# The key group ahead of the indexer's queries, page fetches one megabyte at a time, and a bit search that picks one of two prepared words

## The chip, the core and the metric

The kernel runs on one core of one Trainium2 chip. The time is device microseconds of one execution; lower is better. The kernel before was timed in three runs; a profiled execution, with its own time, gives the rows further down.

## The reference

One inference step of a two-layer decoder runs for 256 prompt tokens and for 8 sample sequences of 4 new tokens each, 288 tokens in all. Layer 0 mixes tokens by sparse attention, layer 1 by a Conformer convolution; each is followed by a convolutional FFN. Only the attention layer is touched here. Cut to what matters:

```python
p = x @ w_in            # 2048 -> q 2048 | k 512 | v 512 | qi 1024 | ki 64 | wi 16
q, k, qi, ki = partial rotary of each
dots  = einsum('thd,sd->ths', qi, ki)                      # 16 index heads of 64
score = einsum('th,ths->ts', wi * scale, relu(dots))
idx   = top_k(where(causal, score, -inf), k_sel)           # 64 of 256 (prompt), 256 of 2052 (sample)
o     = softmax(q . k[idx]) v[idx];  y = o @ w_out
```

For the samples `ki` consists of 2048 cached rows per sequence, on 16 pages of 128 rows that a page table names, and 4 new ones. The cached keys and values are gathered by the selected index.

## The kernel before

All activations stand transposed, features on partitions and the 288 tokens along the row. Every weight GEMM is done in three fp32r matmuls per tile: weights and activations are each split into a high and a low part, and the products high-high, low-high and high-low are summed in PSUM (lines 227 to 229). A `Slab` is 512 KB of weights. `pump` (line 134) works ahead of PE: it issues slab loads on SP's queue up to five ahead into the `raw` ring, and splits slabs up to two beyond the current one: `wh` on ACT (line 158), `wl` as raw minus wh on VectorE (line 160), or on GpSimd where `s.pool` is set. That is so for the first two of the four attention query groups (lines 545 to 547). PE, ACT, VectorE, GpSimd and SP each run what they are given in order.

The order is written by hand, by credits. `gemm` yields after some matmuls the PE time that they stand for (0.3675 for three), and `tick` (line 166) adds it to each of several `Lane`s: `ev` (what follows a group's evacuation), `bg` (page loads, then the sample's index work), `bg2` (preparations and the first half of the prompt's index). A lane is a queue of generators; while its credit is positive its next piece is emitted into the engines' programs, and the number that the piece yields is taken off the credit. So a `yield 1.4` says: give PE 1.4 us of GEMM before the next piece. A credit is capped at 3. `drain` emits at once whatever is left in a lane. With `k.fine` set, GEMMs tick after every three or six matmuls, otherwise after each column block.

The attention layer's groups come in this order: an 80-column group (`ki` and `wi`), two groups of index queries `qi`, the group of keys `k`, four groups of queries `q`, two of `v`. A 512-column group is 8 slabs, 192 matmuls, 23.52 credits. `k.fine` is set ahead of the `k` group.

Around them:

- **Pages.** Lines 658 to 669: four indirect gathers on GpSimd's DMA queue each bring 1 MB of index pages (128 pages, a quarter of the features) into a `kvt` tile, and four stores put them into a DRAM buffer `kid`. The program order on GpSimd is gather 0, 1, 2, store 0, gather 3, store 1, 2, 3; a store waits for its gather. `load_kx` (line 671) then reads `kid` back, transposed, in eight loads of 512 KB issued on ACT, one per sequence; each needs all four stores. The first comes after `KXD[0]` = 30 credits, the others `KXD[1]` = 3 apart.
- **Index of the samples.** `sample_index` (line 801) follows `load_kx` in `bg`. It waits until the second `qi` group is rotated (`rope_qi`, line 697), does all dots with the cached rows (line 833), and sums them into a score row `S` of 516 columns on 128 partitions (four strips of each of 32 tokens).
- **The search.** Lines 878 to 895 find each token's 256th largest score, bit by bit, 31 bits. One bit is: count the scores at or above the candidate (line 881, VectorE, with an accumulator), sum the four strips by a PE matmul (`total`, line 861), compare with 256 into `fb`, the bit's value if the count suffices (line 893, from PSUM), and candidate `nx ^ fb` (line 895). Beside that `v ^ fb` (line 884) and the next `nx` (line 888) are made. `v`, `nx`, `fb`, `cand` are words of 128x1.
- **Compaction.** Lines 896 to 980: ties are ranked, the selected columns are moved together in nine predicated steps (lines 938 to 946) and shifted by strip in eight (lines 965 to 972); a PE matmul adds the strips (line 975), `idxS` is written (line 978), and `kv_load` starts gathers of keys and values. Then the second half of the prompt's index goes on (`prompt_index(1)`, line 985): 16 top-k rounds on VectorE (lines 1029 to 1033), 8 over 128 and 8 over 256 columns, 2.6 credits each.
- **Keys and queries.** `evac_rope` (line 704) copies a group's PSUM out on ACT and puts the rotation into `ev`. The `k` group also stores its output through SP.

After the four `q` groups everything left is drained (line 1068), then come the two `v` groups (line 1085) and the attention loop over 32 sample tokens. The rest of the kernel follows in one stream of GEMMs.

Of the kernel before, what the change touches and what calls it, by code (L numbers as in the profile page):

```python
# [7 lines left out]
F32 = mybir.dt.float32  # L8
# [9 lines left out]
NT = 16  # L18
# [27 lines left out]
CQ = 287  # L46
KXD = (30.0, 3.0)
PEM, NACT = 3, 4
BIS = (1.4, 0.2)
ROPE = 0.5  # L50
# [482 lines left out]
def trunk(ctx, tc, a, o, stages=9):  # L533
# [5 lines left out]
    win, wout = a["w_attn_in"], a["w_attn_out"]  # L539
    g_idx = [k.add(Group([(win, KIC, 80)], [80], NT, 8))]  # L540
    g_idx += [k.add(Group([(win, QIC + 512 * i, 512)], [128] * 4, NT, 2)) for i in range(2)]
    g_k = k.add(Group([(win, KC, 512)], [128] * 4, NT, 2))
    g_q = [k.add(Group([(win, QC + 512 * i, 512)], [128] * 4, NT, 2)) for i in range(4)]
# [120 lines left out]

    for i in range(6):
        if i < 4:
            gather(kx[i], kq, pgq[:, i:i + 1])
        if i >= 2:
            nc.gpsimd.dma_start(kid[:, 2048 * i - 4096:2048 * i - 2048], kx[i - 2])

# [130 lines left out]
    def sample_index():  # L801
# [47 lines left out]
        nc.vector.tensor_copy(S[:, :512], sc[:, :512])  # L849
        yield 1.5  # L850
        p = pb()
# [26 lines left out]
        for bit in range(30, -1, -1):  # L878
            cnt = sp.tile([128, 1], F32, name="cnt", bufs=2)
            scr = sp.tile([128, W1], I16, name="scr", bufs=2)  # L880
            nc.vector.tensor_scalar(scr, S, cand.bitcast(F32), 0.0, op0=OP.is_ge, op1=OP.add, accum_out=cnt)
            if bit < 30:
                w = word("v")
                nc.vector.tensor_tensor(w, v, fb, op=OP.bitwise_xor)
                v = w
            if bit:
                nx = word("nx")
                nc.vector.tensor_scalar(nx, v, 1 << (bit - 1), None, op0=OP.bitwise_xor)
            yield BIS[0]
            p = total()  # L890
            yield BIS[1]
            fb = word("fb")
            nc.vector.tensor_scalar(fb, p[:, :1], float(KSEL_S), float(1 << bit), op0=OP.is_ge, op1=OP.mult)
            cand = word("cand")
            nc.vector.tensor_tensor(cand, nx if bit else v, fb, op=OP.bitwise_xor)
        v = cand
# [41 lines left out]
        for b in range(9):  # L938
            s_ = 1 << b
            m = sp.tile([128, 512], I32, name="m_", tag="w", bufs=3)  # L940
            nc.vector.tensor_scalar(m, x_, 1 << (15 + b), None, op0=OP.bitwise_and)
            y = sp.tile([128, 512], I32, name="x_", tag="w", bufs=3)
            nc.vector.scalar_tensor_tensor(y, m, 0.0, x_, op0=OP.is_equal, op1=OP.mult)
            nc.vector.copy_predicated(y[:, :512 - s_], m[:, s_:], x_[:, s_:])
            x_ = y
            yield 2.2

# [15 lines left out]
        nc.vector.tensor_copy(lst, xi)  # L963
        yield 2.2
        for b in range(8):
# [5 lines left out]
            lst = y  # L971
            yield 1.2
        p = pb()
# [65 lines left out]

    k.bg2.append(prepare())  # L1040
    for gi in range(2):
        ps = k.gemm(g_idx[gi + 1], xin, pg)
# [3 lines left out]
        if gi == 0:  # L1046
# [4 lines left out]

    k.fine = True
    kT = ap.tile([128, NKV, T], F32, name="kT")
    vt = ap.tile([128, 2, 512], F32, name="vt")
    vs = ap.tile([32, 512], F32, name="vs")
    q = base.tile([128, NT, T], F32, name="x")
    qn = ap.tile([128, NKV, NS * TS, GQ], F32, name="qn")
    ps = k.gemm(g_k, xin, pg)
    evac_rope(0, ps, [kT[:, m] for m in range(4)],
              lambda: nc.sync.dma_start(o["k"].rearrange("(j p) t -> p j t", p=128), kT))  # L1060

# [793 lines left out]
```

## Time and profile before

| | |
|---|---|
| three runs, median (lowest to highest) | 2680.12 us (2676.99 to 2683.59) |
| the profiled execution, its own time | 2690.26 us |
| its span | 2688.5 us |
| PE busy | 2565.7 us (95%) |
| VectorE (DVE) busy | 1650.9 us (61%) |
| ScalarE (ACT) busy | 1160.8 us (43%) |
| GpSimd (POOL) busy | 619.6 us (23%) |
| DMA | 454.90 MB, 169 GB/s on the mean |

PE is the matmul stream, PEld its weight loads, which overlap it. The busy share of PE says little about a single stage: its idle stretches are short and lie mostly in the attention layer, so the rows below are taken from the first 345 us. "Idle before" in brackets names what ended an engine's idle time. A letter q behind an engine (SPq, ACTq) marks its DMA issues. The granted clock is a share of PE's full clock: 1.00 is the higher of its two levels, 0.50 the lower. Matmul records are missing here and there.

### The profile page before, as it was taken

Reading aid. Unit: us, or ns where it says so; the run is one execution under the profiler, and the core shown is the slowest. Engines: PE = TensorE matmul, PEld = TensorE weight load, DVE = VectorE, ACT = ScalarE, POOL = GpSimd, SP = SyncE. Lnnn points to the kernel's source line nnn. Section 1 sums busy time; section 2 is a strip of 40 time slices with the busy share of each in tenths; the row PEclk is TensorE's granted clock in tenths of the full one; section 3 lists DMA queues with packets and bytes.
Section 4 is the critical chain, followed back from the end, with each engine's and each line's share of the span. In section 5 each row is a group of like instructions: output and inputs, shape, how many; then the busy total and the mean of one; then the engine's idle time right before and its main releaser. Section 6 shows DMA issues by size and latency. Waiting matters only on the chain.

```text
span 2688.5 us, 49542 instructions
## 1 busy us (share of the span) xinstructions
PE 2565.7 (95%) x19608; PEld 2460.0 (92%) x19608; DVE 1650.9 (61%) x2544; ACT 1160.8 (43%) x1801; POOL 619.6 (23%) x857
## 2 busy tenths in 40 slices
PE   6888888999999999999999999899999999999997
PEld 5677865999999999999999889899999999999997
DVE  4479643668566445555557888778655544555554
ACT  3333343446444334444345544656444333444334
POOL 2023233143122110101135454443111000111123
PEclk8899999999999999999999999999999999999998
DMA  9533666555554555555544767455555445555643
GB/s 325 118 103 117 226 219 232 176 162 184 181 161 154 176 162 168 161 172 159 170 159 132 195 159 184 165 163 157 173 162 168 163 160 165 171 166 159 171 164 106
DMA packets 410552, 454.90 MB, mean 169 GB/s; under 512 B 34816, under 2 KB 338608, under 8 KB 409168
## 3 DMA queue, kind: packets, MB, share of 16 engines
q1 hardware_dynamic: 389600, 396.46, 47.8%
q0 software_dynamic: 12400, 51.09, 5.6%
q10 hardware_dynamic: 8320, 4.19, 0.8%
q8 instruction: 153, 2.51, 0.4%
q14 instruction: 79, 0.65, 0.1%
HBM read 438.37 MB, written 13.30 MB: 168 GB/s over the span
## 4 chain that ended last, share of the span: by engine, by line
PE 79%; DVE 3%; POOL 2%; issue 1%; ACT 1%; DMA 1%; SPq 0%; ACTq 0%; DVEq 0%; POOLq 0%
PE pt L229 25%; PE pt L228 25%; PE pt L227 25%; PE tr L1181 1%; PE pt L1641 1%; DVE wl L160 1%; PE m L1245 1%; PE sc L1202 1%; POOL x L485 0%; PE q L1153 0%; ACT wh L158 0%; DMA xt<-spread 0%; PE tr L1131 0%; DMA kvx<-kvc,idxS 0%; DVE cy L1687 0%
## 5 line engine op out<-in xcount | busy, mean ns | idle before, releaser
L160 DVE TENSOR_TENSOR wl<-raw,wh 128x1024 fp32r<-128x1024 f32 (+2 forms) x709 | 885.3, 1251 | 795.1 <-ACT wh L158 781.8
L158 ACT ACTIVATE wh<-raw 128x1024 fp32r<-128x1024 f32 (+1 forms) x726 | 760.5, 1051 | 949.7 <-PE pt L228 692.7
L229 PE MATMUL pt<-xh,wl 128*128 128x288 f32 (+1 forms) x3520 | 1040.5, 296 | 4.8 <-DVE wl L160 4.8
L227 PE MATMUL pt<-xh,wh 128*128 128x288 f32 (+1 forms) x3520 | 1042.6, 296 | 0.8 <-ACT xh L1300 0.8
L228 PE MATMUL pt<-xl,wh 128*128 128x288 f32 (+1 forms) x3520 | 1042.7, 296 | 0.1
L229 PEld LDWEIGHTS pt<-xh,wl 128*128 128x128 f32 x3520 | 666.5, 189 | 6.4 <-DVE wl L160 6.4
L227 PEld LDWEIGHTS pt<-xh,wh 128*128 128x128 f32 x3520 | 663.7, 189 | 7.8 <-issue 5.3
L228 PEld LDWEIGHTS pt<-xl,wh 128*128 128x128 f32 x3520 | 664.1, 189 | 0.5 <-DVE xl L1301 0.3
L229 PE MATMUL pt<-hh,wl 128*128 128x288 f32 (+1 forms) x1664 | 495.5, 298 | 2.9 <-DVE wl L160 2.9
L227 PE MATMUL pt<-hh,wh 128*128 128x288 f32 (+1 forms) x1664 | 493.2, 296 | 1.2 <-ACT wh L158 1.2
L228 PE MATMUL pt<-hl,wh 128*128 128x288 f32 (+1 forms) x1664 | 494.1, 297 | 0.0
L229 PEld LDWEIGHTS pt<-hh,wl 128*128 128x128 f32 x1664 | 312.8, 188 | 3.9 <-DVE wl L160 3.9
L227 PEld LDWEIGHTS pt<-hh,wh 128*128 128x128 f32 x1664 | 313.5, 188 | 2.3 <-ACT wh L158 2.1
L228 PEld LDWEIGHTS pt<-hl,wh 128*128 128x128 f32 x1664 | 313.8, 189 | 0.2
L1416 POOL COPY sto<-gpad 128x2 f32<-128x2 f32 x88 | 82.0, 931 | 963.5 <-ACT gpad L1409 963.4
L227 PE MATMUL pg<-xh,wh 128*128 128x288 f32 (+1 forms) x464 | 144.1, 311 | 15.9 <-ACT wh L158 13.7
L229 PE MATMUL pg<-xh,wl 128*128 128x288 f32 (+1 forms) x464 | 140.3, 302 | 3.7 <-DVE wl L160 3.2
L228 PE MATMUL pg<-xl,wh 128*128 128x288 f32 (+1 forms) x464 | 140.2, 302 | 0.1
L1420 ACT ACTIVATE s<-y,pvec 128x304 f32<-128x304 f32 x88 | 48.4, 550 | 162.0 <-DVE y L1415 162.0
L227 PEld LDWEIGHTS pg<-xh,wh 128*128 128x128 f32 (+1 forms) x464 | 89.3, 193 | 19.2 <-ACT wh L158 14.1
L302 POOL TENSOR_TENSOR lns<-lns,x 128x288 f32<-128x288 f32 x56 | 52.8, 944 | 184.3 <-DVE x L1329 176.8
L229 PEld LDWEIGHTS pg<-xh,wl 128*128 128x128 f32 (+1 forms) x464 | 89.3, 192 | 5.6 <-DVE wl L160 5.6
(386 smaller groups left out, 2447.5 us busy)
## 6 DMA issues: line engine op xcount, KB each, us to landing
raw<-w_ffn_gate SPq DMA_DIRECT2D x352, 256.0 KB, 2.9
raw<-w_ffn_up SPq DMA_DIRECT2D x352, 256.0 KB, 3.2
raw<-w_ffn_down SPq DMA_DIRECT2D x169, 512.0 KB, 3.6
raw<-w_attn_in SPq DMA_DIRECT2D x64, 512.0 KB, 4.3
raw<-w_pw SPq DMA_DIRECT2D x128, 256.0 KB, 4.7
raw<-w_attn_out SPq DMA_DIRECT2D x32, 512.0 KB, 4.7
raw<-w_pw SPq DMA_DIRECT2D x32, 512.0 KB, 4.2
xt<-spread SPq DMA_DIRECT2D x60, 136.0 KB, 2.8
```

The lines of the kernel that those rows point to most:

```text
L158: nc.scalar.activation(wh[:, :n], r[:, :n], AF.Copy)
L160: eng.tensor_tensor(wl[:, :n], r[:, :n], wh[:, :n].bitcast(F32), op=OP.subtract)
L227: nc.tensor.matmul(out, wh[:, c:c + w], xh, start=st, stop=False)
L228: nc.tensor.matmul(out, wh[:, c:c + w], xl, start=False, stop=False)
L229: nc.tensor.matmul(out, wl[:, c:c + w], xh, start=False, stop=sp)
L302: nc.gpsimd.tensor_tensor(self.s1, self.s1, self.x[:, j], op=OP.add)
L1181: nc.tensor.transpose(p[:, h * 128:(h + 1) * 128], g[:, h * 128:(h + 1) * 128], ident)
L1202: nc.tensor.matmul(p[32 * h:32 * h + 16, :KSEL_S], qz[b % 2][:, i, h], kt[:, h], start=False, stop=(i == TS - 1), skip_group_check=True)
L1245: nc.tensor.matmul(po[32 * h:32 * h + 16, :128], z[:, c, i, h], g[:, 512 + h * 128:640 + h * 128], start=False, stop=(i == TS - 1 and c == ...
L1416: nc.gpsimd.tensor_copy(sto[:, j, 0:2], gp[:, 256:258])
L1420: nc.scalar.activation(s[:, :304], y[:, :304], AF.Silu, bias=k.par(bc, j))
L1641: nc.tensor.matmul(p[32 * i:32 * i + 32, :TP], dg[:, i, m - PEM], xt[:, i, 4 * (m - PEM):4 * (m - PEM) + TP], start=m == PEM, stop=m == 7, ...
```

## The change

Three things are edited, and the credits with them.

1. The group of keys comes right behind the 80-column group, in the list of slabs (so in the order of weight loads) and in the program; `k.fine` and the tiles of keys and values move up with it. The two index-query groups follow, then the four query groups. `sample_index` now starts beside the first query group.
2. On GpSimd's queue each page gather is followed at once by its store, so the order is gather 0, store 0, gather 1, store 1, and so on. The first read-back comes after 42 credits, the others 4.2 apart.
3. In the search, two candidates are made from the current one by XOR with constants, one for each outcome of the bit's test; the test's flag picks by a predicated copy. `v` and the product with the bit's value are gone.

The credits: 1.3 for 1.4 in the search's first wait of a bit, 0.5 for 1.5 behind the score sum, 2.4 for 2.2 per compaction step, 1.2 for 2.2 ahead of the list, 1.3 for 1.2 per list step.

```diff
-KXD = (30.0, 3.0)
+KXD = (42.0, 4.2)
-BIS = (1.4, 0.2)
+BIS = (1.3, 0.2)
...
     g_idx = [k.add(Group([(win, KIC, 80)], [80], NT, 8))]
+    g_k = k.add(Group([(win, KC, 512)], [128] * 4, NT, 2))
     g_idx += [k.add(Group([(win, QIC + 512 * i, 512)], [128] * 4, NT, 2)) for i in range(2)]
-    g_k = k.add(Group([(win, KC, 512)], [128] * 4, NT, 2))
...
-    for i in range(6):
-        if i < 4:
-            gather(kx[i], kq, pgq[:, i:i + 1])
-        if i >= 2:
-            nc.gpsimd.dma_start(kid[:, 2048 * i - 4096:2048 * i - 2048], kx[i - 2])
+    for i in range(4):
+        gather(kx[i], kq, pgq[:, i:i + 1])
+        nc.gpsimd.dma_start(kid[:, 2048 * i:2048 * i + 2048], kx[i])
...
         nc.vector.tensor_copy(S[:, :512], sc[:, :512])
-        yield 1.5
+        yield 0.5
...
             nc.vector.tensor_scalar(scr, S, cand.bitcast(F32), 0.0, op0=OP.is_ge, op1=OP.add, accum_out=cnt)
-            if bit < 30:
-                w = word("v")
-                nc.vector.tensor_tensor(w, v, fb, op=OP.bitwise_xor)
-                v = w
-            if bit:
-                nx = word("nx")
-                nc.vector.tensor_scalar(nx, v, 1 << (bit - 1), None, op0=OP.bitwise_xor)
+            below = 1 << bit >> 1
+            no, yes = word("no"), word("yes")
+            nc.vector.tensor_scalar(no, cand, 1 << bit | below, None, op0=OP.bitwise_xor)
+            nc.vector.tensor_scalar(yes, cand, below, None, op0=OP.bitwise_xor)
             yield BIS[0]
             p = total()
             yield BIS[1]
-            fb = word("fb")
-            nc.vector.tensor_scalar(fb, p[:, :1], float(KSEL_S), float(1 << bit), op0=OP.is_ge, op1=OP.mult)
-            cand = word("cand")
-            nc.vector.tensor_tensor(cand, nx if bit else v, fb, op=OP.bitwise_xor)
+            fl = word("fl")
+            nc.vector.tensor_scalar(fl, p[:, :1], float(KSEL_S), None, op0=OP.is_ge)
+            nc.vector.copy_predicated(no, fl, yes)
+            cand = no
...
             nc.vector.copy_predicated(y[:, :512 - s_], m[:, s_:], x_[:, s_:])
             x_ = y
-            yield 2.2
+            yield 2.4
...
         nc.vector.tensor_copy(lst, xi)
-        yield 2.2
+        yield 1.2
...
             lst = y
-            yield 1.2
+            yield 1.3
...
     k.bg2.append(prepare())
+
+    k.fine = True
+    kT = ap.tile([128, NKV, T], F32, name="kT")
+    vt = ap.tile([128, 2, 512], F32, name="vt")
+    vs = ap.tile([32, 512], F32, name="vs")
+    qn = ap.tile([128, NKV, NS * TS, GQ], F32, name="qn")
+    ps = k.gemm(g_k, xin, pg)
+    evac_rope(0, ps, [kT[:, m] for m in range(4)],
+              lambda: nc.sync.dma_start(o["k"].rearrange("(j p) t -> p j t", p=128), kT))
+
     for gi in range(2):
         ps = k.gemm(g_idx[gi + 1], xin, pg)
...
     k.bg.append(sample_index())
 
 
-    k.fine = True
-    kT = ap.tile([128, NKV, T], F32, name="kT")
-    vt = ap.tile([128, 2, 512], F32, name="vt")
-    vs = ap.tile([32, 512], F32, name="vs")
     q = base.tile([128, NT, T], F32, name="x")
-    qn = ap.tile([128, NKV, NS * TS, GQ], F32, name="qn")
-    ps = k.gemm(g_k, xin, pg)
-    evac_rope(0, ps, [kT[:, m] for m in range(4)],
-              lambda: nc.sync.dma_start(o["k"].rearrange("(j p) t -> p j t", p=128), kT))
```

## Rows read from the trace of the kernel before

**Rows 1.** The page's part 4, the chain that ended last: share of the span by engine.

```profile
PE 79%; DVE 3%; POOL 2%; issue 1%; ACT 1%; DMA 1%; SPq 0%; ACTq 0%; DVEq 0%; POOLq 0%
```

**Rows 2.** Busy time in six stretches. Columns: stretch (us), its length, then for PE, PEld, DVE, ACT and POOL the busy us with the number of instructions, the granted PE clock, the DMA share, GB/s.

```profile
18.00:55.60 37.60, 30.54 (x201) 28.76 (x200) 15.77 (x26) 11.91 (x15) 11.10 (x20) 0.91 1.01 399
72.00:95.00 23.00, 23.00 (x175) 23.00 (x174) 8.41 (x9) 7.23 (x8) 0.00 (x0) 1.00 1.00 209
95.00:109.50 14.50, 4.11 (x28) 3.46 (x27) 9.22 (x18) 2.92 (x6) 0.00 (x0) 0.72 0.96 213
144.00:229.50 85.50, 68.94 (x493) 64.56 (x491) 73.54 (x203) 27.78 (x42) 33.61 (x15) 1.00 0.38 116
229.50:280.00 50.50, 41.74 (x303) 40.49 (x304) 47.13 (x83) 18.07 (x27) 6.13 (x4) 0.99 0.42 126
280.00:286.00 6.00, 6.00 (x27) 6.00 (x28) 1.66 (x4) 2.66 (x6) 0.00 (x0) 0.53 0.30 87
```

**Rows 3.** The DMA queues in four stretches, in this order: q1 in 16 to 20 us, q0 in 22 to 23 us (its first packets), q0 and q1 in 36 to 40 us, q0 in 49 to 50 us (its last packets). q0 is GpSimd's, q1 is SP's. Columns: packets, MB, share of 16 engines.

```profile
q1 hardware_dynamic: 596, 1.62, 103.5%
...
q0 software_dynamic: 33, 0.27, 65.8%
...
q0 software_dynamic: 184, 1.37, 81.0%
...
q1 hardware_dynamic: 181, 0.35, 22.5%
...
q0 software_dynamic: 2, 0.00, 1.2%
```

**Rows 4.** GpSimd in order of time, 0 to 60 us: the first page gather, the first store, the last gather, the last store. Columns: start, length, engine, line, operation; in brackets the idle time before it and what ended that.

```profile
17.81 1.04 POOL L654 DMA_INDIRECT kvt<-kiT,pgq  x1 [14.34 <-DVE pgq L662]
...
27.92 0.58 POOL L669 DMA_DIRECT2D kid<-kvt  x1 [6.55 <-DMA kvt<-kiT,pgq]
...
28.80 1.63 POOL L654 DMA_INDIRECT kvt<-kiT,pgq  x1 [0.30 <-DVE identN L798]
...
40.57 0.53 POOL L669 DMA_DIRECT2D kid<-kvt  x1 [5.71 <-DMA kvt<-kiT,pgq]
```

**Rows 5.** ACT in order of time, 50 to 100 us: the first and the last page load, and the evacuation of the second query group.

```profile
54.86 0.66 ACTq L674 DMA_DIRECT2D kvt<-kid  x1
...
94.62 4.33 ACTq L674 DMA_DIRECT2D kvt<-kid  x1
...
99.00 1.32 ACT L1044 ACTIVATE qi<-pg 128x288 f32<-128x288 f32 x4 [3.34 <-issue]
```

**Rows 6.** PE in order of time, 95 to 112 us: the two waits ahead of the dots.

```profile
99.46 0.40 PE L227 MATMUL pg<-xh,wh 128*128 128x288 f32 x1 [1.43 <-ACT qi L1044]
...
109.49 2.90 PE L833 MATMUL pg<-kvt,qiblk 128*128 128x512 f32 x3 [8.97 <-issue]
```

**Rows 7.** VectorE in the same stretch: the split ahead of the rotation, and the copies behind it.

```profile
101.29 1.22 DVE L160 TENSOR_TENSOR wl<-raw,wh 128x1024 fp32r<-128x1024 f32 x1 [4.37 <-ACT wh L158]
...
108.36 0.92 DVE L808 COPY qiblk<-qi 64x128 f32<-64x128 f32 x4
```

**Rows 8.** GpSimd and VectorE in order of time, 162 to 219 us: two of GpSimd's splits, and what VectorE began inside each.

```profile
162.86 2.40 POOL L160 TENSOR_TENSOR wl<-raw,wh 128x1024 fp32r<-128x1024 f32 x1 [117.10 <-ACT wh L158]
...
163.21 2.07 DVE L884 TENSOR_TENSOR v<-v,fb 128x1 int32<-128x1 int32 x1
...
218.42 2.36 POOL L160 TENSOR_TENSOR wl<-raw,wh 128x1024 fp32r<-128x1024 f32 x1 [0.39 <-ACT wh L158]
...
218.53 0.75 DVE L881 TENSOR_SCALAR_CACHE_REDUCE scr<-S,cand 128x516 int16<-128x516 f32 x1
```

**Rows 9.** Groups of instructions in 162.5 to 229.5 us on VectorE (the two XORs, the compare) and on GpSimd (the splits). Columns: line, engine, operation, out<-in, count | busy us, mean ns of one | idle before.

```profile
L884 DVE TENSOR_TENSOR v<-v,fb 128x1 int32<-128x1 int32 x24 | 16.0, 668 | 0.0
...
L895 DVE TENSOR_TENSOR cand<-nx,fb 128x1 int32<-128x1 int32 x23 | 14.5, 631 | 0.8
...
L893 DVE TENSOR_SCALAR fb<-pg 128x1 int32<-128x1 f32 x24 | 3.7, 155 | 5.1 <-PE pg L863 5.1
...
L160 POOL TENSOR_TENSOR wl<-raw,wh 128x1024 fp32r<-128x1024 f32 x14 | 33.3, 2378 | 150.1 <-ACT wh L158 148.4 <-PE pg L863 1.8
```

**Rows 10.** Groups by shape in 140 to 345 us: the widest and the narrowest predicated copy.

```profile
L944 DVE COPY_PREDICATED x__2146<-m__2144,x__2121 128x511 int32<-128x511 int32 x1 | 0.7, 745 | 0.0
...
L944 DVE COPY_PREDICATED x__2387<-m__2385,x__2358 128x256 int32<-128x256 int32 x1 | 0.5, 464 | 0.0
```

**Rows 11.** The end of the stage: PE's wait for the index list (229.5 to 286 us), VectorE in order of time (first flushed round, the mask behind the last, the next split), PE's wait for that split, and the two halves of a narrow top-k round as groups.

```profile
PE pg L975 <- DVE lst L968: 3.5, 1, 3.5
...
312.49 0.42 DVE L1031 MAX8 m<-pacc 128x8 f32<-128x256 f32 x1
...
319.37 0.23 DVE L1035 TENSOR_SCALAR pm<-pacc 128x128 bf16<-128x128 f32 x1
...
319.71 3.49 DVE L160 TENSOR_TENSOR wl<-raw,wh 128x1024 fp32r<-128x1024 f32 x3
...
320.99 0.40 PE L229 MATMUL sc<-xh,wl 128*128 128x288 f32 x1 [0.48 <-DVE wl L160]
...
L1031 DVE MAX8 m<-pacc 128x8 f32<-128x128 f32 x8 | 2.3, 288 | 0.0
...
L1032 DVE MATCH_REPLACE8 pacc<-m,pacc 128x128 f32<-128x128 f32 x8 | 2.2, 276 | 0.0
```

## The prediction

> **What bounds the kernel now.** I read the chain of waits first: the tensor engine (PE) alone holds 79% of it [rows 1]. So the change can only matter where PE stands still, and all it edits lies before about 345 us. Next I read busy time by stretch there [rows 2]. At full flow PE issues 175 matmuls in 23.0 us, 0.1314 us each; with that pace each stretch shows its loss. 18.0 to 55.6 us (first query group): 201 matmuls are worth 26.4 us, so 11.2 are lost. 95 to 109.5 us (before the index dots): 28 are worth 3.7, so 10.8 are lost. 144 to 229.5 us is the bit search, 229.5 to 280 the compaction, both with VectorE busy 86 and 93%. The DMA queues, the engines' timelines and the waits then say why [rows 3 to 11].
>
> **Part 1: the front.** From 22 us the pages' queue (q0) and the weights' queue (q1) are both loaded; in 36 to 40 us they move 184 and 181 packets, almost one for one, and since q0's are larger q1 gets 0.35 MB in 4 us, 88 GB/s, against 1.62 MB when alone [rows 3]. PE eats 512 KB per 24 matmuls = 3.15 us, 166 GB/s, so it starves: that is the 11.2 us. The change doesn't cut the bytes. It lets only one gather and the store before it be in flight, because a store now waits on GpSimd ahead of the next gather. Gather issue to next store issue took 10.1 us, store issue to next gather 0.9 [rows 4], a cycle of 11.0; in it q0 moves 2.1 MB, 6.1 us at 1.37 MB per 4 us. For the other 4.9 us q1 has the engines to itself: (6.1 x 88 + 4.9 x 405) / 11.0 = 229 GB/s, over the 166 needed. I leave 0.7 us of loss and take **-10.5** (bounds: 0, if starving merely lasts longer, and -11.2). K standing there instead of the first queries changes nothing for PE: 192 matmuls, 8 weight loads on SP, 8 splits each on ACT and VectorE, as the group it displaces; its rotation (4 VectorE and 8 ACT pieces) and its 576 KB output store on SP fall into the next group, which has no other work on the lane.
>
> What waits behind the stores on GpSimd: the index output, three memsets, four copies and four products for later use; their first reader is the dots near 100 us. But the page loads on ACT wait for the last store too. Stores issue at 27.9, 38.9, 49.9, 60.9; the last store of the kernel before was issued at 40.57 and its data ended within 49 to 50 us [rows 3, 4], 8.4 later, so now 69.3. A lower bound: the first gather needed 4.4 us from issue to data beside a full q1 [rows 3, 4]; if a quiet q1 saves 2.4 of that in each trip and in the last store, the cycle is 8.6 and the end 59.7. The first load comes after 42 credits: 5.9 of the 80-column group, 23.5 of K, 12.6 = 103 matmuls = 13.5 us into the queries, that is 43.9 + 13.5 = 57.4 us. (The same rule puts it just behind the first query group in the kernel before, where it is, at 54.86 [rows 5].) ACT then stands still, and the weight splits behind the load with it. Two slabs beyond the current one are split by then, so PE has work to 43.9 + 7 x 3.15 = 66.0; after ACT is free it needs 0.6 for the issue and 2.3 for a split. At an end of 60 the cost is 0, at 69.3 it is 69.3 + 2.9 - 66.0 = 6.2 plus 2.4 of low clock (below). Nearer the middle, 65: **+2**.
>
> **Part 2: before the dots.** Before, the eighth load held ACT from 94.62 for 4.33 us, so the query evacuation came at 99.00 although PE had finished the group near 95; then VectorE waited for a split until 101.29, rotated to 108.4, and PE's dots began at 109.49 after waits of 1.43 and 8.97 [rows 5 to 7]. Now the loads stand 4.2 credits apart instead of 3.0 and end 5 credits before the group does, so ACT evacuates at once: end + 0.5. Q0's split is on GpSimd, not ahead of the rotation; but it reads SBUF for 2.4 us and holds up one of the rotation's products by about 1.1 (part 3). Rotation and copies took 7.0 from that split's end to the dots; end + 0.5 + 7.0 + 1.1 = end + 8.6, with 6 matmuls of cover (0.8): lost 7.8 against 10.8, **-3.0** (bounds -5 and 0).
>
> **Part 3: the search.** 31 bits, each a count over 516 columns, a PE sum, a compare and the next candidate. Between 162.5 and 229.5 us there are 24 bits in 67.0 us, 2.79 each; a bit's own PE work is 1.6 credits = 1.74 us plus some 0.3 for the sum, 2.05. The difference is GpSimd: 14 weight splits of 2.38 us run there, and the two XORs of 128x1 average 0.668 and 0.631 us instead of 0.16 [rows 8, 9]. One row shows it: GpSimd's split from 162.86 to 165.26, VectorE's XOR from 163.21 to 165.28. The count, begun at 218.53 inside a split, took its usual 0.75 [rows 8]. So VectorE work with two inputs from SBUF waits until GpSimd is done, work with one doesn't. Excess: 24 x 0.513 + 24 x 0.47 + the last, together 25 us, 1.8 per split; half hits the first XOR, half the second, and PE's share of it is (24 x 0.74 - 2.7 for two rotations) / 14 = 1.08 per split. The seven earlier bits (K as cover) lose some 2. Loss now 17.8 + 2 = 19.8.
>
> After: the first XOR is gone, both candidates are one-input, and the pick has mask and data in SBUF. The trace has no 128x1 pick and none beside GpSimd; at 511 and 256 columns it takes 0.745 and 0.464 [rows 10], which runs down to 0.18 at one, as a XOR. I take it that it waits like the XORs. Then a hit at the second XOR costs what it did, a hit at the first 1.76 less the 0.75 us to the next pick, 1.0, where 1.36 counted (0.4 lay beside PE's sum): 0.18 less on the mean, 0.90 per split, x 14 = 12.6; one rotation instead of two 1.35, VectorE splits at the end 1.0: 14.9 against 19.8, **-4.9** (bounds -15, if the pick never waits, and +2, if splits always start just ahead of the pick). The 0.1 credit less per bit only moves 3.5 us of PE work behind the search.
>
> The Trainium skill, "SBUF — State Buffer", section "Who interferes with whom", says that a VectorE instruction with two SBUF inputs contends with a GpSimd instruction that reads SBUF. The XOR rows agree; for the pick no row here shows it, and by the page it would wait, as assumed.
>
> **Part 4: compaction.** It held 50.5 us for 303 matmuls, with VectorE the limit [rows 2]. Now it lies wholly in the two groups whose splits are on VectorE: 3.5 splits x 1.15 and one rotation of 1.8 more, two GpSimd stalls of 1.85 less, 1.5 credits (1.6 us) more PE work taken in: **+0.6** (bounds -2, +4).
>
> **Part 5: the end of the stage.** Five GEMM groups stood beside search and lists before, 117.6 credits; now four, 94.1. Sample work to the index list costs 90.4 credits of 94.9, so 4.5 remain where about 23 did, and 2 of the 16 top-k rounds are paced; 14 are flushed at the end instead of 7. Before, the flush ran from 312.49 to the split at 319.71, and PE waited 0.48 for that split at 320.99 [rows 11]. Seven rounds more are one of 0.98 (312.49 to 319.37 over seven) and six of the narrow ones at 0.66 (0.288, 0.276 and a load of 0.09), with 0.56 of mask work: 5.5 us in which the V group's third slab can't be split. PE stands, then runs at the low clock: after the 3.5 us wait at the list, 280 to 286 us show a granted clock of 0.53, 27 matmuls where 45 fit, 2.4 us lost [rows 2, 11]. 5.5 + 2.4 is about **+8.0** (bounds +3, if PE comes later by itself, +10). The key gathers start with the list as before; between it and their reader stay the two V groups, 192 matmuls or 25 us, and that wait, while 4 MB at q0's 343 GB/s take 12: hidden.
>
> **Sum.** -10.5 + 2.0 - 3.0 - 4.9 + 0.6 + 8.0 = -7.8 us on the profiled 2690.26, whose span is 2688.5. That run is 10.1 above the median of those shown, 2680.12; the same step from the median gives 2672.3.
>
> **Rivals.** *The pick doesn't wait for GpSimd* (17%). Part 3 becomes -15, total -17.9: 2662.2. For it: the count, with one tensor input, passes GpSimd; against: every two-input row that meets a split waits. *The pages come late* (18%), the slower side: the page loads hold ACT, and PE stops with no split weights. Loss is the stores' end - 60.7 us with the low clock; it passes the 9.8 that undo the gain at an end of 70.5, just above my upper bound. With cycles of 15 us (store behind gather on one loaded queue) the end is 81, loss 20, total +10.5: 2690.6. For it: all four trips are now in series. Against: q1 drains in each gap, and gathers get faster then. *Starving only moves* (10%): q0 still wins while it is busy, the loss falls by 4 instead of 10.5, total -1.3: 2678.8.
>
> **How the numbers follow.** Measurement tells 0.3%, 8 us, from nothing. The forecast case has 55% and its own range is 2664 to 2681: it splits 0.29 faster, 0.235 same, 0.025 slower. The free pick adds 0.165 and 0.005; late pages 0.07 same, 0.11 slower; moved starving 0.025, 0.05, 0.025. Together 0.48, 0.36, 0.16. The range reaches from below the free pick, 2652 (with all of part 1), to 2690.
>
> **What would show it.** Right: in the K group near 18 to 44 us almost no PE wait on weight splits; stores on GpSimd about 11 us apart; a dots wait near 8; XOR-like picks of 1 to 2 us, about one per GpSimd split; a flush of 14 top-k rounds and a PE wait of some 6 us in the V group. Wrong: a page load on ACT that ends past 70 us, picks that always take 0.2, or no wait in V.

## The result, and the profile after

The changed kernel takes 2658.96 us (median of 5 runs, 2655.23 to 2659.64) where the kernel before, run beside it, takes 2677.15 (5 runs): ratio 0.9925, 95% interval 0.9907 to 0.9942. That is 18 us won; 7.8 were predicted. A second comparison (below) gave 0.9943 (0.9929 to 0.9957). The level of the kernel before differed between the sets of runs (2677.2, 2689.5, 2690.6, 2678.6, 2676.6 us), so ratios are compared, each to the kernel before in its own set.

The profiled run has 2659.64 us. Its page, busy time and the chain by engine (the chain answers to [rows 1]):

```profile
span 2657.9 us, 49546 instructions
...
PE 2554.7 (96%) x19608; PEld 2457.8 (92%) x19608; DVE 1623.3 (61%) x2546; ACT 1161.7 (44%) x1801; POOL 619.1 (23%) x857
...
PE 85%; DVE 5%; DMA 4%; POOL 2%; issue 2%; ACT 1%; SPq 0%; ACTq 0%; DVEq 0%; POOLq 0%
```

The two profiled runs lie 30.6 us apart, more than the medians. Where, three instants of the traces tell: the index list's matmuls begin at 279.8 us before and 273.8 after; the attention loop's key transposes run from 342.8 to 467.7 before and from 321.6 to 436.2 after; behind the loop they take 2220.8 and 2221.7 us to the end of the span. So 21.2 us are won by the loop's start, all in what the change edits, and 10.3 more in a loop that it doesn't touch. In all other traces of this study that loop takes 112 to 115 us in the sets whose kernel before is at 2677 to 2679, and 122 to 128 in the sets at 2690, whatever the kernel; the profiled run of before, 13 us over its set's median, had a loop of 124.9. It isn't the change's: the changed kernel itself had 114.6 us here and 124.0 when run again (f0 below). The sets ran on different chips: those at 2689.5 and 2690.6 on chips 8 and 5, those at 2678.6 and 2676.6 on chips 7 and 10; for the first set no number is on record. So the chip may be the reason. That wasn't tested, and why the loop has two lengths stays open. The loop's start is therefore the second yardstick below. It comes from one trace of each kernel, and the two traces of the changed kernel differ by 1.9 us in it (321.6 and 319.7).

Busy time by stretch, columns as in [rows 2]:

```profile
17.60:43.00 25.40, 24.09 (x179) 23.62 (x178) 14.53 (x25) 9.84 (x11) 5.30 (x5) 1.00 1.04 401
43.00:76.50 33.50, 30.66 (x211) 29.49 (x211) 12.38 (x14) 13.51 (x24) 7.52 (x15) 0.95 0.94 307
...
157.80:223.60 65.80, 60.43 (x457) 59.56 (x457) 46.95 (x205) 25.90 (x41) 31.55 (x15) 1.00 0.43 129
223.60:275.20 51.60, 46.39 (x332) 45.54 (x331) 47.97 (x87) 18.92 (x26) 0.69 (x2) 0.96 0.44 130
275.20:321.00 45.80, 36.90 (x242) 35.88 (x242) 27.14 (x72) 15.64 (x25) 16.70 (x16) 0.86 0.71 251
```

At 0.1314 us a matmul, K's group (first line) loses 1.9 us, the first query group behind it (second line) 5.8. The third line is the bit search. It took 85.5 us for 493 matmuls and now takes 65.8 for 457; 36 matmuls fewer are 4.7 us, so 15 us of loss are gone. VectorE was busy 86% of it and is busy 71%. Its groups there, columns as in [rows 9], and then GpSimd's splits:

```profile
L889 DVE COPY_PREDICATED_SCALAR no<-fl,yes 128x1 int32 x31 | 6.7, 217 | 1.1
L888 DVE TENSOR_SCALAR fl<-pg 128x1 int32<-128x1 f32 x31 | 4.9, 157 | 13.6 <-PE pg L861 13.6
L882 DVE TENSOR_SCALAR no<-no 128x1 int32<-128x1 int32 x30 | 4.5, 149 | 0.0
L883 DVE TENSOR_SCALAR yes<-no 128x1 int32<-128x1 int32 x30 | 4.3, 144 | 0.0
```

```profile
L160 POOL TENSOR_TENSOR wl<-raw,wh 128x1024 fp32r<-128x1024 f32 x13 | 31.1, 2389 | 53.8 <-ACT wh L158 53.8
```

The pick isn't the operation of [rows 10]: with one element a partition it is a form of its own, COPY_PREDICATED_SCALAR. The 31 of them take 0.216 to 0.220 us each, and 22 begin inside one of the 13 splits of 2.39 us; the XORs averaged 0.668 and 0.631 [rows 9]. In order of time, a pick well inside a split (VectorE's row, GpSimd's row):

```profile
161.15 0.22 DVE L889 COPY_PREDICATED_SCALAR no<-fl,yes 128x1 int32 x1
```

```profile
159.66 2.39 POOL L160 TENSOR_TENSOR wl<-raw,wh 128x1024 fp32r<-128x1024 f32 x1 [37.97 <-ACT wh L158]
```

It doesn't wait. The idle time of VectorE now stands before `fl`, 13.6 us of it, waiting for PE's sum: PE sets the pace in most of the search.

The front: GpSimd's page stores, then SP's longest waits in 40 to 60 us (engine, what it waited for: total, times, longest), then ACT in order of time:

```profile
27.66 0.55 POOL L667 DMA_DIRECT2D kid<-kvt  x1 [9.14 <-DMA kvt<-kiT,pgq]
39.35 0.56 POOL L667 DMA_DIRECT2D kid<-kvt  x1 [9.28 <-DMA kvt<-kiT,pgq]
50.66 0.55 POOL L667 DMA_DIRECT2D kid<-kvt  x1 [8.73 <-DMA kvt<-kiT,pgq]
60.24 0.55 POOL L667 DMA_DIRECT2D kid<-kvt  x1 [7.74 <-DMA kvt<-kiT,pgq]
```

```profile
SPq L1044 <- ACT kT L718: 11.4, 1, 11.4
```

```profile
63.82 1.06 ACT L158 ACTIVATE wh<-raw 128x1024 fp32r<-128x1024 f32 x1 [7.94 <-DMA raw<-w_attn_in]
68.63 0.65 ACTq L672 DMA_DIRECT2D kvt<-kid  x1
```

The stores stand 11.7, 11.3 and 9.6 us apart (predicted 11.0), and the issue of the first page load ends before 70 us. But K's 576 KB output store on SP waits 11.4 us for K's last copy, the weight loads queue behind it, and ACT has nothing to split until 63.82.

PE's waits from 10 to 345 us, which answer to [rows 6] and [rows 11]:

```profile
PE pg L1000 <- DVE wtok L989: 8.1, 1, 8.1
PE pg L831 <- issue: 6.9, 1, 6.9
PE sc L229 <- DVE wl L160: 6.3, 1, 6.3
PE pg L861 <- DVE yes L883: 4.5, 2, 3.6
PE pg L970 <- DVE lst L963: 3.6, 1, 3.6
```

The dots' wait is 6.9 (8.97 and 1.43 before), the list's 3.6 (3.5), and the V group's wait on its split has grown from 0.48 to 6.3, behind this on VectorE, where 14 top-k rounds run in one piece from 283.99:

```profile
296.84 0.29 DVE L1031 SCALAR_TENSOR_TENSOR pm<-pacc,con 128x128 bf16<-128x128 f32 x1
297.04 3.49 DVE L160 TENSOR_TENSOR wl<-raw,wh 128x1024 fp32r<-128x1024 f32 x3
```

### The profile page after: what moved, and what is told of

It reads as the page before. It is cut to its first block, busy times and chain, and to the rows that moved or that the text cites. A ratio compares the mean times of both kernels' runs of the same rounds, so it can differ in the third digit from the quotient of the medians.

```text
span 2657.9 us, 49546 instructions
## 1 busy us (share of the span) xinstructions
PE 2554.7 (96%) x19608; PEld 2457.8 (92%) x19608; DVE 1623.3 (61%) x2546; ACT 1161.7 (44%) x1801; POOL 619.1 (23%) x857
## 4 chain that ended last, share of the span: by engine, by line
PE 85%; DVE 5%; DMA 4%; POOL 2%; issue 2%; ACT 1%; SPq 0%; ACTq 0%; DVEq 0%; POOLq 0%
PE pt L229 25%; PE pt L228 25%; PE pt L227 25%; DVE wl L160 2%; PE pg L227 1%; DMA kvt<-kiT,pgq 1%; PE pg L228 1%; PE pg L229 1%; PE pt L1638 1%; PE tr L1178 1%; ACT wh L158 1%; DMA kvt<-kvc,idxS 1%; PE pg L831 1%; PE pg L1000 1%; DMA xt<-spread 1%
```

## The experiments

All runs with their ratio to the kernel before in the same set, and three instants of the profiled run (first matmul each): the prompt dots behind the first query group, the index list, the attention loop's start.

| run | median us (before beside it) | ratio (95%) | dots | list | loop |
|---|---|---|---|---|---|
| kernel before, its profile | | | 63.3 | 279.8 | 342.8 |
| changed, first comparison | 2659.0 (2677.2) | 0.9925 (0.9907 to 0.9942) | 85.2 | 273.8 | 321.6 |
| e1_old_step | 2692.1 (2689.5) | 1.0017 (1.0006 to 1.0028) | 84.8 | 295.7 | 340.3 |
| e2_step_alone | 2675.2 (2689.5) | 0.9947 (0.9935 to 0.9960) | 62.9 | 262.3 | 326.1 |
| e3_kstore_act | 2676.3 (2689.5) | 0.9944 (0.9929 to 0.9959) | 86.1 | 274.7 | 324.9 |
| e4_old_pages | 2679.8 (2689.5) | 0.9961 (0.9949 to 0.9974) | 90.4 | 281.5 | 330.6 |
| f0_changed_again | 2674.2 (2690.6) | 0.9943 (0.9929 to 0.9957) | 84.2 | 272.0 | 319.7 |
| f1_late_loads | 2675.4 (2690.6) | 0.9943 (0.9928 to 0.9958) | 79.4 | 271.8 | 320.0 |
| f2_wide_pick | 2693.8 (2690.6) | 1.0005 (0.9995 to 1.0015) | 82.4 | 293.6 | 345.2 |
| f3_v_first | 2666.4 (2690.6) | 0.9911 (0.9897 to 0.9925) | 84.5 | 272.8 | 318.8 |
| g1_loads_placed | 2654.5 (2678.6) | 0.9913 (0.9895 to 0.9930) | 79.6 | 267.5 | 315.1 |
| g2_together | 2646.7 (2678.6) | 0.9878 (0.9861 to 0.9895) | 79.8 | 271.0 | 313.0 |
| g3_order_alone | 2692.2 (2678.6) | 1.0051 (1.0036 to 1.0066) | 89.5 | 306.8 | 353.2 |
| h1_no_k_ahead | 2645.2 (2676.6) | 0.9885 (0.9868 to 0.9903) | 53.8 | 254.7 | 306.5 |

### The bit step: e1, e2, f2

e1 is the changed kernel with the old bit step put back; e2 is the kernel before with the new one alone:

```
-            below = 1 << bit >> 1
-            no, yes = word("no"), word("yes")
...
-            nc.vector.copy_predicated(no, fl, yes)
+            nc.vector.tensor_tensor(w, v, fb, op=OP.bitwise_xor)
...
+            nc.vector.tensor_tensor(cand, nx if bit else v, fb, op=OP.bitwise_xor)
```

> The changed kernel with the bit step of the kernel before (two XORs of two tensors, 1.4 credits), all else as changed. In the trace of the changed kernel the search takes 65.7 us for 457 matmuls where it took 85.5 for 493; 36 matmuls fewer are 4.7 us, so 15.1 us less are lost. Theory A, the pick never waits for GpSimd, and that alone gives these 15 us: 2672 to 2675 us (+13 to +16 on the median of 2659), XORs of about 2 us back in the search. Theory B, my predicted term, the step gives only 4.9 and the rest comes from the order (one rotation fewer in the search): 2663 to 2665 us.

> The kernel before with the new bit step alone (1.3 credits), queries before K and pages as before. Theory A, the pick never waits: -13 to -16 us on the median of 2677, so 2661 to 2664; the front stays as slow as it was. Theory B (-4.9): 2672. If order and pages matter for nothing on the whole, this comes out level with the changed kernel, 2659.

e1 is at 1.0017 against 0.9943 for the changed kernel: the step is worth 0.0074 x 2690 = 20 us in the new order (25 by the first comparison's 0.9925), 20.6 by the loop's start (340.3 against 319.7). e2 gains 14.3 us on the kernel before (16.7 by the loop's start). Theory A holds and B (4.9) falls; in the new order the step is worth more than A said. To the loop's start PE's listed waits come to 53.7 us in e1 and 38.5 in the changed kernel (f0), which are A's 15; the rest lies in the granted clock, 0.93 there against 0.94. e1's XORs wait again, and e2's picks take 0.217 us:

```profile
L893 DVE TENSOR_TENSOR cand<-nx,fb 128x1 int32<-128x1 int32 x30 | 19.2, 640 | 1.0
L882 DVE TENSOR_TENSOR v<-v,fb 128x1 int32<-128x1 int32 x30 | 12.0, 399 | 0.0
```

e2 says one thing more. At 0.9947 it is level with the changed kernel's 0.9943 (0.9925 in the first comparison, where 0.0022 is 6 us; 6.4 us by the loop's start). So the step by itself brings most of the gain, and order, pages and credits together add 1 to 6 us to it.

f2 asks whether the pick escapes because it is predicated or because it has one element a partition:

```
-            no, yes = word("no"), word("yes")
+            no, yes = word("no", 2), word("yes", 2)
+            c2 = cand[:, :1].to_broadcast([128, 2])
...
-            cand = no
+            cand = no[:, :1]
```

> The changed kernel with candidates, flag and pick of 128x2 instead of 128x1, both columns alike, so that the pick is a plain predicated copy of a tensor and not the form with one element a partition. Theory A, a predicated copy with mask and data in SBUF waits for GpSimd's splits, and only the one-element form doesn't: picks of 1 to 2 us beside splits, +8 to +12 us on the changed kernel. Theory B, no predicated copy waits here: picks of about 0.2 us throughout and a time within 2 us of the changed kernel's.

It loses 19.7 us on the changed kernel by the medians of their set, 17 by the ratios and 25.5 by the loop's start: about as much as the old step. VectorE in the same search as groups, then in order of time with the two GpSimd splits of that stretch:

```profile
L890 DVE COPY_PREDICATED no<-fl,yes 128x2 int32<-128x2 int32 x31 | 21.9, 707 | 1.1
L883 DVE TENSOR_SCALAR no<-no 128x2 int32<-128x2 int32 x30 | 10.6, 352 | 0.0
```

```profile
169.20 1.89 DVE L883 TENSOR_SCALAR no<-no 128x2 int32<-128x2 int32 x1
...
172.94 1.76 DVE L890 COPY_PREDICATED no<-fl,yes 128x2 int32<-128x2 int32 x1
```

```profile
168.67 2.38 POOL L160 TENSOR_TENSOR wl<-raw,wh 128x1024 fp32r<-128x1024 f32 x1 [3.65 <-ACT wh L158]
172.30 2.38 POOL L160 TENSOR_TENSOR wl<-raw,wh 128x1024 fp32r<-128x1024 f32 x1 [1.24 <-ACT wh L158]
```

Both rows end with the split beside them, 171.05 and 174.68. A plain predicated copy waits, as I had assumed; the one-element form doesn't. And an instruction with one tensor input, `no`, waits as well once it has two elements: 0.149 us became 0.352 on the mean. f2 overturns my "work with one doesn't" (wait) as a general rule, and its loss is that of two waits, the pick's and `no`'s. Nor is one element a partition enough by itself: the XORs of two tensors wait at 128x1 [rows 8, 9]. The Trainium skill, "SBUF — State Buffer", section "Who interferes with whom", says that a tensor_scalar can enter a mode in which it too contends with GpSimd. The Trainium skill, "VectorE: DVE Perf Modes", section "Mode 2×_2P", asks for an outermost dimension above one that is even, or odd and equal in input and output, for that mode. The 128x2 and 128x1 rows agree. The prediction took the first page's rule on two SBUF inputs to cover the pick; the one-element form, at 0.217 us, doesn't follow it, and neither page speaks of that form.

### The front: e4, e3, f1, g1

e4 puts the old gathers back, two ahead of the stores:

```
-    for i in range(4):
-        gather(kx[i], kq, pgq[:, i:i + 1])
-        nc.gpsimd.dma_start(kid[:, 2048 * i:2048 * i + 2048], kx[i])
+    for i in range(6):
...
+            nc.gpsimd.dma_start(kid[:, 2048 * i - 4096:2048 * i - 2048], kx[i - 2])
```

> The changed kernel with the pages fetched as before: gathers run two ahead of the stores. Theory A, my predicted term: K's group starves again as the first query group did before, 201 matmuls in 37.6 us instead of 26.4, +8 to +10.5: 2667 to 2670 us. Theory B, starving was only moved, from the pages to the wait on SyncE's queue: K's group loses some 10 us again, the first query group wins about 8 back, since the pages are through by 50 us: 2657 to 2662 us.

4.8 us slower than the changed kernel by the ratios (0.0018), 10.9 by the loop's start; the expected 8 to 10.5 lie between. K's group starves again, 122 matmuls in the 25.4 us that held 179:

```profile
17.60:43.00 25.40, 19.41 (x122) 17.89 (x121) 10.38 (x22) 5.59 (x6) 8.38 (x14) 0.90 1.03 419
```

By the time alone theory B isn't excluded (2679.8 - 0.9943 x 2689.5 is +5.6, B allowed +3); that starving falls on whichever group stands there is shown, that it is wholly moved is not.

e3 takes K's store off SP's queue:

```
-              lambda: nc.sync.dma_start(o["k"].rearrange("(j p) t -> p j t", p=128), kT))
+              lambda: nc.scalar.dma_start(o["k"].rearrange("(j p) t -> p j t", p=128), kT))
```

> The changed kernel with K's 576 KB output store issued on ScalarE's queue, which has made K's copies itself, and not on SyncE's, where it waited 11.4 us for them with the weight loads behind it. Theory A, this wait starves the first query group (PE waits 8.2 us for wh near 57 to 65 us): that wait goes, 2650 to 2652 us (-7 to -9). Theory B, the pages' traffic starves PE wherever it falls, and the store's place in the queue is nothing: 2657 to 2661. Theory C, the wait goes, but then ScalarE reaches the first page load some 8 us earlier (about 60 us) and stands there until the last page store ends near 67: 2655 to 2659 with a first load on ScalarE that is long, and PE without split weights at 63 to 70 us.

I had misread one row here: the PE wait of 8.2 us on `wh` is the kernel's first matmul at 8 us. From 15 to 76 us PE's listed waits come to 4.1, and with low clock and short gaps the first query group loses 6.0: 43.0 to 77.1 us are worth 259 matmuls and hold 214. So 6 us, not 8, were there to be won, and e3 won none (ratio 0.9944). ACT in its trace:

```profile
52.70 0.43 ACTq L1044 DMA_DIRECT2D out_k<-kT  x1
...
68.72 0.66 ACTq L672 DMA_DIRECT2D kvt<-kid  x1
69.50 1.06 ACT L158 ACTIVATE wh<-raw 128x1024 fp32r<-128x1024 f32 x1 [10.28 <-DMA out_kidx<-ki]
```

Theory C: SP now issues weights without a stop, but ACT reaches the first page load at 59.2 and stands 10.28 us until the last page store has ended, with the splits behind it (the row names the index output, which was issued right behind that store on the same queue). One wait had hidden the other. f1 takes both away, with `KXD = (52.0, 3.2)` on top of e3:

> K's store on ScalarE's queue as in the run before of that name, and the page loads on ScalarE ten credits (some 10 us) later, 3.2 credits apart, so that ScalarE no longer stands from 59 to 69 us at a load that waits for the last page store. Theory A, the two waits (SyncE's queue, then ScalarE's) took each other's place, and with both gone PE's wait of 8 us in the first query group goes: 0.989 to 0.990 of the kernel before (-7 to -10 us on the changed one). Theory B, the weights starve anyway, since the page queue and K's store leave the weights' queue 0.15 MB in 52 to 60 us: PE still waits 5 us or more there, 0.992 to 0.993.

The group does end 4.8 us earlier (dots 79.4 against 84.2), and PE's waits from 15 to 76 us shrink to 1.6. Yet the list stands where it was. g1 is f1 with `KXD = (50.4, 3.15)`, the sample's lane free at the old credit:

> K's store on ScalarE's queue and the page loads from 50.4 credits on, 3.15 apart, so that the lane of the sample's work is free at the same credit as in the changed kernel (42 + 8 x 4.2 = 75.6 = 50.4 + 8 x 3.15); in the run with late loads it was 77.6. That run ended the first query group 4.8 us earlier (prompt dots at 79.3 us against 84.1) and had nothing of it left at the index list (271.8 against 272.0). Theory A, its two credits of delay moved the search and the lists against the GEMM groups and ate the gain: now 3 to 5 us on the changed kernel stay (0.9925 to 0.9932). Theory B, time won in the front is lost again in the search whatever the credits, since that is paced by VectorE and GpSimd: 0.994 again, the list near 272.

0.9913, and now the gain is still there at the list (267.5 against 272.0) and at the loop (315.1 against 319.7). That fits theory A, and the gain was larger than it said; but that the two credits ate it in f1 is argued, not shown. f1 and g1 ran in different sets: against the changed kernel g1's 0.9913 is 8 us by 0.9943 and 3 by 0.9925. And g2 below, whose program is g1's up to the list, reaches the list at 271.0, so that instant differs by 3.5 us between traces of the same work. What separates f1 and g1 to the loop's start is the granted clock (columns as in [rows 2], for PE alone; f1, then g1):

```profile
10.00:320.00 310.00, 271.94 (x1816) 0.93 0.60 191
10.00:315.10 305.10, 268.50 (x1815) 0.95 0.61 194
```

0.07 x 310 and 0.05 x 305 us differ by an estimated 6 us of full speed, within the rounding the 4.9 between the two, while PE's listed waits are nearly the same (37.9 and 36.3 us). Over the whole span f1's five runs show a clock of 0.982 to 0.985, those of the changed kernel beside it 0.984 to 0.987. Whether the two credits brought the low clock about, no run shows.

### The end of the stage, and the order: f3, g2, g3, h1

f3 runs V's first group ahead of the drain and paces the rounds through it:

```
-TOPK = 2.6
+TOPK = 1.0
...
+    ps_v0 = k.gemm(g_v[0], xin, pg)
+    vT0 = R[:, 2:4]
...
     k.drain(k.ev, k.bg2, k.bg)
```

> The changed kernel with V's first group multiplied ahead of the final drain, in the PSUM banks of this stage, with top-k rounds of 1.0 credit between its matmuls instead of 14 rounds in one piece before it. Theory A, my predicted term: the wait of 6.3 us on V's split and the low clock behind it go, -6 to -9 us on the changed kernel. Theory B, the end of this stage is hidden, since the attention loop waits for its keys or its own chain: PE reaches the loop earlier and waits there, -2 to +2.

By the times theory A, 7.8 us won (0.0032). The trace shows less: the 6.3 us are gone, but the second V group now waits for the first one's last transposed copy, and the loop starts only 0.9 us earlier than in f0 (whose profiled run was the fastest of its five; 2.8 us earlier than in the first trace). What the flush costs is thus between 1 and 8 us here; why the two readings differ stays open.

```profile
PE m L227 <- DVE vs L1076: 4.6, 1, 4.6
```

g2 is f3 and g1 together, with six unused bank allocations (`pg()`) ahead of V's first group:

> The run before together with V's first group ahead of the drain, and that group's PSUM banks turned by six, so that V's second group doesn't wait 4.6 us for the last transposed copy. If the gains add (-7.8 for V first, -3 to -5 for the front, -2 to -4 for the banks): 0.987 to 0.989 of the kernel before. If the front's gain is lost in the search and the loop behind V waits for its keys instead: 0.991, as V first alone.

0.9878: the gains add. From list to loop it takes 42.0 us where g1 takes 47.6, but with its later list the loop starts only 2.1 us earlier than in g1. The bank turn didn't do what it was for: 3.2 us of the wait for `vs` remain.

g3 has the old bit step and the old pages, so that K ahead, the later page loads and the other altered credits are left:

> The changed kernel with the old bit step and the old pages: what is left of the change is K ahead of the queries, the page loads' later place and the altered credits. Theory A, the order by itself costs, through the flush of top-k rounds (7.8 us back in the run with V first) and the queue waits: slower than the kernel before by 5 to 11 us (1.002 to 1.004). Theory B, as I predicted part by part (-3.0 + 0.6 + 8.0, and one rotation fewer in the search): +3 to +6 (1.001 to 1.002). Theory C, K ahead is a gain by itself: below 0.998.

+13.6 us, more than either theory. PE's longest waits in its trace, 10 to 352 us:

```profile
PE pg L863 <- DVE scr L881: 11.9, 13, 1.5
PE pg L1005 <- DVE wtok L994: 8.1, 1, 8.1
PE sc L229 <- DVE wl L160: 7.3, 1, 7.3
PE pg L833 <- issue: 6.9, 1, 6.9
```

Of these only the third is new against before (0.48), and in total the listed waits to the loop's start hardly grow, from 54.2 to 56.0 us, while the loop starts 10.4 us later. What does change is the granted clock (columns as in [rows 2], for PE alone; before, then g3):

```profile
10.00:342.80 332.80, 277.97 (x1815) 0.94 0.57 178
10.00:353.20 343.20, 286.81 (x1819) 0.91 0.56 173
```

By estimate, 0.06 x 333 us are some 20 us of full speed lost to the lower level, 0.09 x 343 some 31. All five runs of g3 agree: 0.980 or 0.981 over the span, where the kernel before beside them has 0.983 to 0.987. So most of the loss is low clock and not waiting. The lower level, 0.50, is granted from within a wait on into the work behind it: from 85.6 to 105.9 us around the 8.1 us wait for `wtok` (dots at 89.5), from 324.5 to 334.6 around the 7.3 us in the V group. Why these stretches add up to more than before, no run shows.

h1 goes the other way: no K ahead, but the new step, the new pages, `KXD = (54.0, 2.4)` and K's store on ACT. The compaction's and the list's credits are those of the kernel before:

> The order of the kernel before (both query groups, then K) with the new bit step, the pages one megabyte at a time, page loads from 54 credits on (about 69 us, when the last page store has ended), 2.4 apart, and K's store on ScalarE's queue. Theory A, K ahead earns nothing by itself: the order alone cost 0.5%, so without it the step (-0.5%) and a front that doesn't starve (first query group over by about 45 us and not 55.5) add up, the dots stand beside K's group, and the time is 0.985 to 0.989 of the kernel before. Theory B, K ahead is what buys the time for the pages; without it the dots wait for pages that come 15 us later than before, or their loads starve K's weights: 0.992 to 0.996, no better than the step alone.

0.9885, level with g2 and better than the changed kernel: theory A. Its first stretch, columns as in [rows 2] for PE alone, then its longest waits:

```profile
18.00:43.40 25.40, 24.15 (x179) 1.00 1.04 404
```

```profile
PE pg L1000 <- DVE wtok L989: 7.7, 1, 7.7
PE sc L229 <- DVE wl L160: 7.1, 1, 7.1
PE pg L970 <- DVE lst L963: 3.6, 1, 3.6
```

The first query group no longer starves (it ends at 46.1 us, 55.6 before), K's group covers the wait for the dots, which is gone from the list, and the loop starts 36.3 us earlier than before. The nearest kernel with K ahead is g1; h1 is 0.0028 (7.5 us) better, 8.6 by the loop's start. The two differ in the order, in `KXD` and in the other credits, so this difference isn't the order's alone. The V group's 7.1 are still in it; V first on top of h1 wasn't tried.

## Why the prediction was right and wrong

The direction and the range held; the gain was more than twice the forecast, and the rival "the pick doesn't wait for GpSimd" (2662.2) came nearer than the forecast. The measured time lies below the forecast case's own 2664 to 2681 and inside the whole range only because that was drawn to cover this rival. There is luck in it too: 15 us more in part 3 were partly offset by 4 less in part 1. By the loop's start of f0 against before, 23.1 us:

- **Part 1 (-8.5; measured -3.7 to -4.7).** The cycle of 11 us and K's unstarved group came as worked out; h1 shows the same for the query group, 9.5 us earlier where 10.5 were forecast. What failed is the sentence that K's store on SP falls into a group "which has no other work on the lane": it costs no lane work, but it waits 11.4 us and the weights queue behind it. The +2 for page loads on ACT was the right mechanism, hidden behind that wait until e3 removed it. Without starving or waits the group would end at 55.6 - 11.2 + 25.2 = 69.6; it ended at 77.1 (f0 76.1, g1 71.5).
- **Part 2 (-3.0; measured -3.5).** 6.9 us of wait against 10.4 before. Right.
- **Part 3 (-4.9; measured -20).** The step that failed: "I take it that it waits like the XORs". At 128x1 the pick takes 0.217 us beside splits and away from them. As a plain copy it would have gained as little as forecast: f2 is within 5 us of the old step in e1 (0.0012 or 3 us better by the ratio, 4.9 worse by the loop's start), with `no` waiting as well. The bound of -15 held for the old order (e2, -14.3) and was passed in the new one.
- **Part 4 (+0.6; measured -0.2).** From the last sum to the list 41.2 us before, 41.0 after. Right within its bounds.
- **Part 5 (+8.0; measured +1 to +8).** 14 rounds flushed and a V wait of 6.3 us, as worked out; the granted clock in 275.2 to 321 us is 0.86. The wait stands in ten traces (5.1 to 7.3 us), its price in time only within 1 to 8 us.

With 20.6 for the step and 5.8 for V's wait, -4.7 - 3.5 - 20.6 - 0.2 + 5.8 is -23.2, the difference by trace. From the changed kernel's first trace the same sum, with 18.7 for the step and -3.7 for part 1, is -20.3 against -21.2, so the match to a tenth is luck. That the medians give 16 to 18 of it is not explained in full: f0's profiled run was 6 us under its median.

No part asked what the order earns by itself. No run shows a gain from it: with the later page loads and the altered credits, but without the new step and pages, it costs 13.6 us (g3), and h1 does better without it. Order and credits weren't separated. Nor did a part price the low clock over the whole stage, which is most of g3's loss.

## What to carry to other kernels

Before pricing an instruction from rows at another width, ask whether the narrow form is the same instruction: with one element a partition the pick and `no` pass GpSimd where two elements wait, while a XOR of two tensors waits at one element too. When a wait is removed, look on the same resource for the next one, and on every queue for what waits ahead of the loads: an output store that waits for its data holds whatever is issued behind it. When a background lane is paced by credits, a load moved by two credits moves all that follows in the lane; compare variants at equal credits. And where the waits don't add up to the loss, compare the granted clock over the same stretch.

## What the runs showed of the hardware

- COPY_PREDICATED_SCALAR, 128x1 with mask and data in SBUF: 0.216 to 0.220 us for all 31, of which 22 begin inside a GpSimd split (changed kernel); COPY_PREDICATED at 128x2: 0.163 alone, up to 2.343 beside splits (f2).
- TENSOR_SCALAR from one SBUF tensor (`no`): 0.147 to 0.152 us at 128x1 throughout (changed kernel), up to 2.287 at 128x2 (f2).
- The attention loop of the changed kernel took 114.6 us in one set of runs and 124.0 in another; over all kernels it took 112 to 115 us in some sets and 122 to 128 in others, on other chips where the chip is on record.
- At nearly equal waits, a stage of some 340 us had a granted clock of 0.94 with one order of groups and credits and 0.91 with another (before and g3); 0.50 was granted for 20.3 us around one wait of 8.1 us (g3).
